# Softmax minus one-hot: each partition owns 64 neighbouring rows, and labels load straight into place

## The chip, the cores and the metric

The kernel runs on one core of one Trainium2 chip. The metric is the device time of one execution in microseconds (us). Before the change three runs took 1247.91, 1247.98 and 1248.11 us; the median is 1247.98 us.

## The reference

For 8 x 1024 = 8192 rows of 8192 float32 logits, the kernel computes the softmax of each row and subtracts 1.0 at the row's label. It is the gradient of the cross entropy with respect to the logits.

```python
logits_max = np.max(logits, axis=-1, keepdims=True)
exp_logits = np.exp(logits - logits_max)
softmax = exp_logits / np.sum(exp_logits, axis=-1, keepdims=True)
...
one_hot[batch_idx, seq_idx, labels] = 1.0
return (softmax - one_hot).astype(np.float32)
```

The labels are passed to the kernel as 64-bit integers. Logits in and gradient out are 268.4 MB each, so each byte of 537 MB is moved once.

## The kernel before

The rows are cut into B = 32 blocks of 256. In a block each of the 128 partitions holds G = 2 neighbouring rows, so block b and partition p hold the rows 256b + 2p and 256b + 2p + 1. One row of one partition is 32 KB. Partition p's rows of a block begin 64 KB after partition p-1's in HBM, and a block is one contiguous run of 8 MB. "Step t" below is one row of every partition (128 rows, 4 MB); there are T = 64 steps, two for each block.

SBUF holds three blocks (SLOTS = 3) in one tile `X` of 128 partitions x 3 slots x 2 rows x 8192 columns. Everything works in place in it. The order of all work is written out by hand: the helper `run` (line 63) issues one instruction, puts the waits on semaphores in front of it and increments a counter. As all instructions go through it, the profile shows L68 for nearly all of them, and they are told apart by engine, operation and tile.

Loads are issued by SyncE (SP) on queue q1. The string `LOADS` says for each block whether it is loaded as two DMAs of one row for each partition ("r", 128 pieces of 32 KB) or as one DMA of both rows ("w", 128 pieces of 64 KB): blocks 0 to 4 and 26 to 31 are "r", the 21 between are "w". A load of block b waits until the stores of block b-3, which used the same slot, have landed. Stores are issued by ScalarE (ACT) on queue q10, one for each step (128 pieces of 32 KB). Both directions run on the same 16 DMA engines.

For each step t the main loop (line 160) does this:

- VectorE (DVE) finds the negated row maximum (`tensor_reduce` into `m`), once the load has landed. It is issued one step ahead.
- ScalarE computes exp(x - max) in place and sums the row into `s`.
- VectorE takes the reciprocal into `r`.
- ScalarE multiplies the row by `r`.
- VectorE compares the tile `iota` (the column numbers, int16, in PSUM) with the row's label, and subtracts the result from the row (`scalar_tensor_tensor`). The label is a scalar for each partition, read from the tile `lab`.
- ScalarE issues the store of step t-1 between its two passes of step t.

Before the loop the constants are prepared. ScalarE issues the load of the labels (line 77) into `lab_raw`, with block b on partition b: 32 partitions x 256 labels. GpSimd (POOL) makes a 32x32 identity with a memset and an affine select (lines 78 to 83), and writes the column numbers with an iota into the last row of slot 2 of `X` (line 86), which is still empty. VectorE casts the labels to float (line 91). TensorE (PE) transposes them in two instructions into PSUM (line 93), one for each row j of a block, so that the labels of a partition's rows come to that partition. VectorE copies them into `lab` (line 97), laid out as [row j, block b], and copies the column numbers into PSUM (line 98). This last copy, `w_iota`, waits for the transposed labels, because they stood in the same PSUM tile, and for GpSimd's iota. The second load of block 2 (SP's sixth DMA) waits for it, since it overwrites the place where the column numbers were made, and VectorE's first row maximum stands behind it in VectorE's order.

Of the kernel before, what the change touches and what calls it, by code (L numbers as in the profile page):

```python
# [7 lines left out]
P = 128  # L8
G = 2
# [8 lines left out]
def kernel(  # L18
# [6 lines left out]
    nc = tc.nc  # L25
    fp32 = mybir.dt.float32
    i32 = mybir.dt.int32
    i16 = mybir.dt.int16
    Act = mybir.ActivationFunctionType
    Alu = mybir.AluOpType  # L30

    x_nv = logits.flatten_outer_dims()
    o_nv = out.flatten_outer_dims()
    N, V = x_nv.shape
    T = N // P
    B = T // G
    lab_bp = labels.rearrange("a b -> (a b)").rearrange("(b q) -> b q", q=G * P)
    x_b = x_nv.rearrange("(b p j) v -> b p j v", p=P, j=G)
    o_b = o_nv.rearrange("(b p j) v -> b p j v", p=P, j=G)

    const = ctx.enter_context(tc.tile_pool(name="const", bufs=1))
    psum = ctx.enter_context(tc.tile_pool(name="psum", bufs=1, space=bass.MemoryType.PSUM))


    X = const.tile([P, SLOTS, G, V], fp32)
    lab_raw = const.tile([B, G * P], labels.dtype)
    lab_f = const.tile([B, G, P], fp32)
    ident = const.tile([B, B], fp32)
    lab = const.tile([P, G, B], fp32)

    m, s, r = (const.tile([P, T], fp32, name=n) for n in ("m", "s", "r"))

    iota = psum.tile([P, V], i16)
    lab_ps = iota[:].bitcast(fp32)[:, :T].rearrange("p (j b) -> p j b", j=G)

    with tc.tile_critical():  # L56
        sem = tc.alloc_semaphore
        got = [[sem(f"got{i}{q}") for q in range(2)] for i in range(SLOTS)]
        put = [[sem(f"put{i}{q}") for q in range(2)] for i in range(SLOTS)]
        lab_got, dve, act, pe, pool = (sem(n) for n in ("lab_got", "dve", "act", "pe", "pool"))  # L60
        count = {}

        def run(engine, waits, counter, method, **operands):

            waits = list(dict.fromkeys(waits))
            for w in waits[:-1]:
                engine.wait_ge(*w)
            instruction = getattr(engine, method)(**operands)  # L68
            for w in waits[-1:]:
                instruction._wait_ge(*w)  # L70
            step = 16 if method == "dma_start" else 1
            instruction.then_inc(counter, step)
            count[counter.name] = count.get(counter.name, 0) + step
            return counter, count[counter.name]


        w_raw = run(nc.scalar, [], lab_got, "dma_start", out=lab_raw[:], in_=lab_bp)
        w = run(nc.gpsimd, [], pool, "memset", ap=ident[:], constant=0.0)
        w_ident = run(
            nc.gpsimd, [w], pool, "affine_select",  # L80
            out=ident[:], in_=ident[:], compare_op=Alu.not_equal, fill=1.0,
            base=0, pattern=[[-1, B]], channel_multiplier=1,
        )

        made = X[:, SLOTS - 1, G - 1, :].bitcast(i16)[:, :V]
        w_made = run(
            nc.gpsimd, [], pool, "iota", out=made, pattern=[[1, V]], base=0, channel_multiplier=0
        )
        step = mybir.dt.size(labels.dtype) // 4
        lab32 = lab_raw[:].bitcast(i32).rearrange("b (p j s) -> b j p s", j=G, s=step)  # L90
        w_lab = run(nc.vector, [w_raw], dve, "tensor_copy", out=lab_f[:], in_=lab32[:, :, :, 0])
        for j in range(G):
            w = run(
                nc.tensor, [w_ident, w_lab], pe, "transpose",
                out=lab_ps[:, j, :], in_=lab_f[:, j, :], identity=ident[:],
            )
        w_turned = run(nc.vector, [w], dve, "tensor_copy", out=lab[:], in_=lab_ps)
        w_iota = run(
            nc.vector, [w_turned, w_made], dve, "tensor_scalar",
            out=iota[:].bitcast(i32), in0=made.bitcast(i32), scalar1=0, scalar2=None, op0=Alu.bitwise_or,  # L100
        )

# [17 lines left out]
        def load(b):  # L120
            loaded[b] = []
            before = stored.get(b - SLOTS, last_made if b == SLOTS - 1 else [])
            for q, piece in enumerate(PIECES[LOADS[b]]):
                ps, js = piece
                free = [w for other, w in before if meets(piece, other)]
                w = run(
                    nc.sync, free, got[b % SLOTS][q], "dma_start",
                    out=X[ps, b % SLOTS, js, :], in_=x_b[b, ps, js, :],
                )
                loaded[b].append((piece, w))  # L130

        def store(t):
            b, j = divmod(t, G)
            stored.setdefault(b, [])
            for q, piece in enumerate(PIECES[STORES[b]]):
                ps, js = piece
                if js.stop != j + 1:
                    continue
                w = run(
                    nc.scalar, [finished[t]], put[b % SLOTS][q], "dma_start",  # L140
                    out=o_b[b, ps, js, :], in_=X[ps, b % SLOTS, js, :],
                )
                stored[b].append((piece, w))


        def row(t):
            return X[:, t // G % SLOTS, t % G, :]

        def row_max(t):
            b, j = divmod(t, G)  # L150
            arrived = [w for piece, w in loaded[b] if meets(piece, (every, slice(j, j + 1)))]
            return run(
                nc.vector, arrived, dve, "tensor_reduce",
                out=m[:, t : t + 1], in_=row(t), axis=mybir.AxisListType.X, op=Alu.max, negate=True,
            )
# [3 lines left out]
        w_max = row_max(0)  # L159
        for t in range(T):  # L160
            x = row(t)
            label = lab[:, t % G, t // G : t // G + 1]
            w = run(
                nc.scalar, [w_max], act, "activation",
                out=x, in_=x, func=Act.Exp, bias=m[:, t : t + 1], scale=1.0, accum_out=s[:, t : t + 1],
            )
            w_sum = run(nc.vector, [w], dve, "reciprocal", out=r[:, t : t + 1], in_=s[:, t : t + 1])
            if t + 1 < T:
                if (t + 1) % G == 0:
                    load((t + 1) // G)  # L170
                w_max = row_max(t + 1)
            if t > 0:
                store(t - 1)

            n = 1 if t + 1 < T else 2
            cols = [slice(i * V // n, (i + 1) * V // n) for i in range(n)]
            scaled = [
                run(
                    nc.scalar, [w_sum], act, "activation",
                    out=x[:, c], in_=x[:, c], func=Act.Copy, bias=0.0, scale=r[:, t : t + 1],  # L180
                )
                for c in cols
            ]
            for c, w in zip(cols, scaled):
                w = run(
                    nc.vector, [w], dve, "scalar_tensor_tensor",
                    out=x[:, c], in0=iota[:, c], scalar=label, in1=x[:, c],
                    op0=Alu.is_equal, op1=Alu.subtract, reverse1=True,
                )
            finished.append(w)  # L190
# [34 lines left out]
```

## Time and profile before

| | |
|---|---|
| median of three runs | 1247.98 us |
| span of the profiled execution, first to last instruction | 1245.7 us |
| median above the span | 2.3 us |
| bytes read and written in HBM | 268.50 MB and 268.44 MB |
| mean rate over the span | 431 GB/s |
| VectorE busy | 1119.2 us, 90% of the span |
| ScalarE busy | 919.1 us, 74% |
| GpSimd busy | 7.4 us |
| TensorE busy | 0.4 us |
| DMA from issue to landing: store, load of one row, load of two rows | 30.8, 26.6 and 33.4 us (medians) |

The times come from the runs, everything else from one execution that was recorded by the profiler. Its own time is its span with what lies around it, and that rest is not in the record; the table therefore sets the span against the median of the runs. A page of the profile has six parts: busy time of each engine, the span in 40 slices, the DMA queues, the chain of work that ended last, the groups of equal instructions with the idle time before them, and the DMA issues. The trace also has a record of each DMA packet, with its queue, size and duration; a packet carries one contiguous piece, and 4-byte packets signal completion.

### The profile page before, as it was taken

To read this page: it belongs to the slowest core of one execution; us is meant where nothing else is said; L and a number is where in the kernel's file an instruction comes from. 1 tells how busy PE (TensorE), PEld (TensorE's weight loads), DVE (VectorE), ACT (ScalarE), POOL (GpSimd) and SP (SyncE) were. 2 spreads that over 40 slices of the span, in tenths; PEclk is the share of its full clock that TensorE was granted. 3 is DMA by queue.
4 is the path that set the end of the run, shared out by engine and by line. 5 is a ranking of instruction groups with operands and counts; after the bars stand their busy time and mean duration, and the time that the engine had idled before them with its cause. 6 is when DMAs were issued, how large, how long until landed. Compare 5 with 4: busy or idle time off the path is not lost.

```text
span 1245.7 us, 592 instructions
## 1 busy us (share of the span) xinstructions
PE 0.4 (0%) x2; PEld 0.3 (0%) x2; DVE 1119.2 (90%) x196; ACT 919.1 (74%) x194; POOL 7.4 (1%) x7
## 2 busy tenths in 40 slices
PE   0000000000000000000000000000000000000000
PEld 0000000000000000000000000000000000000000
DVE  5999998888988889888998888988889999999893
ACT  3888886778776787767877778777777788887772
POOL 2000000000000000000000000000000000000000
DMA  9999999999999999999999999999999999999998
GB/s 406 417 429 433 438 433 442 437 426 427 430 435 445 439 417 442 426 430 437 432 443 438 420 435 432 430 437 450 420 426 437 436 428 432 437 435 429 432 437 386
DMA packets 15460, 536.98 MB, mean 431 GB/s; under 512 B 1728, under 2 KB 1728, under 8 KB 1760
## 3 DMA queue, kind: packets, MB, share of 16 engines
q1 hardware_dynamic: 6192, 268.44, 50.0%
q10 hardware_dynamic: 9264, 268.51, 49.9%
q14 instruction: 4, 0.03, 0.0%
HBM read 268.50 MB, written 268.44 MB: 431 GB/s over the span
## 4 chain that ended last, share of the span: by engine, by line
DMA 59%; DVE 37%; another core or an unknown queue 2%; ACT 1%; DVEq 0%; issue 0%; PE 0%; SPq 0%; ACTq 0%
DMA X<-in_logits_dram 31%; DMA out_dram<-X 27%; DVE m L68 18%; DVE X L68 18%; ACT X L68 1%; DVE iota L68 0%; DVEq L56 0%; DMA lab_raw<-in_labels_dram 0%; DVE lab_f L68 0%; DVE r L68 0%; PE iota L68 0%; SPq L68 0%; ACTq L68 0%; DVE lab L68 0%
## 5 line engine op out<-in xcount | busy, mean ns | idle before, releaser
L68 DVE TENSOR_REDUCE m<-X 128x1 f32<-128x8192 f32 x64 | 555.2, 8675 | 94.3 <-DMA X<-in_logits_dram 94.3
L68 ACT ACTIVATE X<-X,m 128x8192 f32<-128x8192 f32 x64 | 455.9, 7123 | 188.4 <-DVE m L68 188.4
L68 DVE SCALAR_TENSOR_TENSOR X<-iota,lab,X 128x8192 f32<-128x8192 int16 (+1 forms) x65 | 559.7, 8612 | 4.1 <-ACT X L68 4.1
L68 ACT ACTIVATE X<-X,r 128x8192 f32<-128x8192 f32 (+1 forms) x65 | 456.0, 7017 | 115.9 <-DVE r L68 115.9
L68 DVE RECIPROCAL r<-s 128x1 f32<-128x1 f32 x64 | 9.9, 154 | 7.3 <-ACT X L68 7.3
L68 ACT ACTIVATION_READ_ACCUMULATOR X<-X,m 128x1 f32 x64 | 12.0, 187 | 0.0
L68 DVE CAST lab_f<-lab_raw 32x256 f32<-32x256 int32 x1 | 3.7, 3685 | 4.7 <-DMA lab_raw<-in_labels_dram 4.7
L68 POOL IOTA X<- 128x8192 int16 x1 | 6.9, 6944 | 0.0
L68 DVE TENSOR_SCALAR iota<-X 128x4096 int32<-128x4096 int32 x1 | 4.4, 4427 | 0.1
L68 ACT ACT_TABLE_LOAD x1 | 1.3, 1283 | 1.3 <-SPq L56 1.3
L68 DVE COPY lab<-iota 128x64 f32<-128x64 f32 x1 | 0.2, 225 | 0.5 <-PE iota L68 0.5
L68 PE MATMUL iota<-ident,lab_f 32*128 32x32 f32 x2 | 0.4, 300 | 8.5 <-DVE lab_f L68 8.5
L68 PEld LDWEIGHTS iota<-ident,lab_f 32*128 32x128 f32 x2 | 0.3, 196 | 8.4 <-DVE lab_f L68 8.4
L68 POOL TENSOR_SCALAR_AFFINE_SELECT ident<-ident 32x32 f32<-32x32 f32 x1 | 0.2, 204 | 0.1
L68 POOL MEMSET ident<- 32x32 f32 x1 | 0.1, 115 | 0.5 <-SPq L56 0.5
L209 POOL MEMSET const-bfloat16-1.0<- 128x1 bf16 x1 | 0.1, 107 | 0.0
L209 POOL MEMSET const-uint8-127<- 128x1 uint8 x1 | 0.1, 107 | 0.0
L209 POOL MEMSET const-float32-0.0<- 128x1 f32 x1 | 0.1, 104 | 0.2 <-issue 0.2
L209 POOL MEMSET const-float32-1.0<- 128x1 f32 x1 | 0.1, 104 | 0.0
## 6 DMA issues: line engine op xcount, KB each, us to landing
out_dram<-X ACTq DMA_DIRECT2D x64, 4096.0 KB, 30.8
X<-in_logits_dram SPq DMA_DIRECT2D x22, 4096.0 KB, 26.6
X<-in_logits_dram SPq DMA_DIRECT2D x21, 33.4
lab_raw<-in_labels_dram ACTq DMA_DIRECT2D x1, 64.0 KB, 3.8
```

The source lines that it names most:

```text
L68: instruction = getattr(engine, method)(**operands)
L209: nc = _bacc.Bacc("TRN2", target_bir_lowering=False, num_devices=1)
```

## The change

Partition p now owns the 64 neighbouring rows 64p to 64p + 63 (2 MB of HBM), and block b takes the rows 64p + 2b and 64p + 2b + 1 of each partition. Loads, stores, their sizes, their order and their waits stay; their addresses in HBM change. The labels of a partition's rows are 64 neighbouring numbers, so one DMA puts them on their partitions (128 partitions x 64 labels, 512 B each), and one cast brings them into `lab`, now in the order of the steps. The identity, the transposes, their PSUM view and the copy out of PSUM are dropped, and with them the semaphore `pe`.

```diff
-    lab_bp = labels.rearrange("a b -> (a b)").rearrange("(b q) -> b q", q=G * P)
-    x_b = x_nv.rearrange("(b p j) v -> b p j v", p=P, j=G)
-    o_b = o_nv.rearrange("(b p j) v -> b p j v", p=P, j=G)
+    lab_pt = labels.rearrange("a b -> (a b)").rearrange("(p t) -> p t", p=P)
+    x_b = x_nv.rearrange("(p b j) v -> b p j v", p=P, j=G)
+    o_b = o_nv.rearrange("(p b j) v -> b p j v", p=P, j=G)
...
-    lab_raw = const.tile([B, G * P], labels.dtype)
-    lab_f = const.tile([B, G, P], fp32)
-    ident = const.tile([B, B], fp32)
-    lab = const.tile([P, G, B], fp32)
+    lab_raw = const.tile([P, T], labels.dtype)
+    lab = const.tile([P, T], fp32)
...
-    lab_ps = iota[:].bitcast(fp32)[:, :T].rearrange("p (j b) -> p j b", j=G)
...
-        w_raw = run(nc.scalar, [], lab_got, "dma_start", out=lab_raw[:], in_=lab_bp)
-        w = run(nc.gpsimd, [], pool, "memset", ap=ident[:], constant=0.0)
-        w_ident = run(
-            nc.gpsimd, [w], pool, "affine_select",
-            out=ident[:], in_=ident[:], compare_op=Alu.not_equal, fill=1.0,
-            base=0, pattern=[[-1, B]], channel_multiplier=1,
-        )
+        w_raw = run(nc.scalar, [], lab_got, "dma_start", out=lab_raw[:], in_=lab_pt)
...
-        lab32 = lab_raw[:].bitcast(i32).rearrange("b (p j s) -> b j p s", j=G, s=step)
-        w_lab = run(nc.vector, [w_raw], dve, "tensor_copy", out=lab_f[:], in_=lab32[:, :, :, 0])
-        for j in range(G):
-            w = run(
-                nc.tensor, [w_ident, w_lab], pe, "transpose",
-                out=lab_ps[:, j, :], in_=lab_f[:, j, :], identity=ident[:],
-            )
-        w_turned = run(nc.vector, [w], dve, "tensor_copy", out=lab[:], in_=lab_ps)
+        lab32 = lab_raw[:].bitcast(i32).rearrange("p (t s) -> p t s", s=step)
+        w_lab = run(nc.vector, [w_raw], dve, "tensor_copy", out=lab[:], in_=lab32[:, :, 0])
         w_iota = run(
-            nc.vector, [w_turned, w_made], dve, "tensor_scalar",
+            nc.vector, [w_lab, w_made], dve, "tensor_scalar",
...
-            label = lab[:, t % G, t // G : t // G + 1]
+            label = lab[:, t : t + 1]
```

More of the change, by code (lines that the diff above doesn't have):

```diff
@@ L59 @@
         put = [[sem(f"put{i}{q}") for q in range(2)] for i in range(SLOTS)]
-        lab_got, dve, act, pe, pool = (sem(n) for n in ("lab_got", "dve", "act", "pe", "pool"))
+        lab_got, dve, act, pool = (sem(n) for n in ("lab_got", "dve", "act", "pool"))
         count = {}
```

## The prediction

> **What bounds the kernel now.** I read the page from the bottom up: first the DMA queues (part 3) and the slices (part 2), then the chain of work that ended last (part 4), then the groups (part 5).
>
> ```profile
> DMA  9999999999999999999999999999999999999998
> GB/s 406 417 429 433 438 433 442 437 426 427 430 435 445 439 417 442 426 430 437 432 443 438 420 435 432 430 437 450 420 426 437 436 428 432 437 435 429 432 437 386
> ...
> q1 hardware_dynamic: 6192, 268.44, 50.0%
> q10 hardware_dynamic: 9264, 268.51, 49.9%
> ...
> DMA 59%; DVE 37%; another core or an unknown queue 2%; ACT 1%; DVEq 0%; issue 0%; PE 0%; SPq 0%; ACTq 0%
> ```
>
> The loads (q1) and the stores (q10) each take half of all sixteen DMA engines' time: 99.9% together. No slice has slack. VectorE's 37% of the chain is not a second bound. In the groups its row maxima stand idle for 94.3 us in front of loads:
>
> ```profile
> L68 DVE TENSOR_REDUCE m<-X 128x1 f32<-128x8192 f32 x64 | 555.2, 8675 | 94.3 <-DMA X<-in_logits_dram 94.3
> ...
> L68 DVE CAST lab_f<-lab_raw 32x256 f32<-32x256 int32 x1 | 3.7, 3685 | 4.7 <-DMA lab_raw<-in_labels_dram 4.7
> L68 POOL IOTA X<- 128x8192 int16 x1 | 6.9, 6944 | 0.0
> L68 DVE TENSOR_SCALAR iota<-X 128x4096 int32<-128x4096 int32 x1 | 4.4, 4427 | 0.1
> ```
>
> So the time is bytes divided by what the DMA engines move, and the question is how long a packet takes. In the trace's packet records a packet is one piece of a partition: 32 KB for one row (2816 loads, 8192 stores), 64 KB for two (2688 loads). Median: 1213 ns for 32 KB, 2418 ns for 64 KB. Added over the records and divided by 16 engines, loads take 621.9 us, stores 621.1 us, together 1243.0 us of the 1245.7 us span; 2.7 us are left for the start, the completion packets (9 ns each) and the labels. The median run of 1247.98 us lies 2.3 us above the profiled span, and I keep these 2.3 us.
>
> If every packet had its median, loads would fall by 2.1 us. **Nothing in the data path can gain more than about 2 us** unless 1213 ns itself falls, and in no record does a 32 KB packet take less.
>
> **The start, part by part.**
>
> *Removed:* on GpSimd a memset (115 ns) and an affine select (204 ns); on TensorE two transposes with their weight loads (0.43 us in the chain); on VectorE one copy (225 ns). These stood in the chain from the labels' landing (4.69 us) to the iota copy's start (9.25 us).
>
> *Changed:* the cast turns from 32x256 into 128x64. The old one took 3685 ns, far above the 225 ns of the 128x64 copy beside it, and ended at 8.40 us, 0.15 us after GpSimd's iota (1.31 to 8.25 us). The trace doesn't say whether the iota held it up. Bounds for the new one: 0.2 us to 3.7 us. It hardly matters: the iota copy also waits for GpSimd's iota, which starts some 0.35 us earlier and ends at about 7.9 us; labels plus cast end between 4.9 and 8.4 us. So the iota copy starts at 7.9 to 8.4 us instead of 9.25, and ends at 12.3 to 12.8 instead of 13.67.
>
> *What is late next:* the first load. It was issued at 0.96 us and took 12.2 us to land, so row 0 is there at 13.2 us. The first maximum can move from 13.6 to 13.2 us and no further: 0.4 us. Behind it only SP's sixth load waits for the iota copy (10.1 us of SP's waiting). Five loads of 4 MB are ahead of it in the queue, 20.97 MB, or 49 us at 431 GB/s; issued 1 us earlier it lands no earlier. As the DMA engines are full to the end, the 0.4 us don't reach the end of the program: I take 0, bounds 0 and -0.4 us.
>
> *Labels:* the same 64 KB come as 128 packets of 512 B instead of 32 of 2 KB. A 2 KB packet took 81 to 315 ns (mean 114), a 4 B packet 9. The 96 more packets cost each engine between 6 x 9 ns = 0.05 us and 6 x 114 ns = 0.7 us: I take 0.3 us. If that delays the labels from 4.7 to 5.4 us, GpSimd's iota still covers it.
>
> *Unmoved:* SP's and ACT's issues stand in the old order with the old waits; every load has its old shape and count, so the packets keep their sizes (the two rows of a 64 KB packet remain neighbours in HBM).
>
> The start is thus worth -0.4 to +0.7 us, 0.3 us taken.
>
> **The address of every packet.** This is the change that counts, and the trace of before has no row for it. Partition p's packet used to lie 64 KB behind that of partition p-1; a block was one run of 8 MB. Now it lies 64 rows x 32 KB = 2 MB behind it, in loads and in stores. All packets of a DMA start at addresses that differ by multiples of 2 MB, so if HBM serves some addresses in turn and not side by side, sixteen engines at the same offset now meet there, and go on meeting in every packet.
>
> The nearest rows are the two places where loads were slow in before. The first sixteen load packets, one for each engine, started within 0.67 us and took 1372 to 2113 ns, mean 1673: 1673/1213 = 1.38. At 48 to 52 us, just after the first store had been issued, 32 load packets took 1380 to 2279 ns, mean 1794: 1.48. The windows show both as a dip while the engines stay busy:
>
> ```profile
> 2.00:4.00 2.00, 0.00 (x0) 0.00 (x0) 0.00 (x0) 0.63 (x1) 2.00 (x1) 1.00 1.04 337
> ...
> 48.00:50.00 2.00, 0.00 (x0) 0.00 (x0) 2.00 (x1) 2.00 (x1) 0.00 (x0) 1.00 0.94 262
> 50.00:52.00 2.00, 0.00 (x0) 0.00 (x0) 2.00 (x1) 2.00 (x1) 0.00 (x0) 1.00 0.86 262
> ...
> 200.00:900.00 700.00, 0.00 (x0) 0.00 (x0) 627.12 (x110) 517.15 (x109) 0.00 (x0) 1.00 1.00 434
> ```
>
> (The last two columns are the DMA share and GB/s.) Stores were never slow: the longest of 8192 took 1291 ns. Bounds for the 2 MB distance are therefore 1.00 (as in nearly all rows) and 1.48 on every packet. I take the row of engines that start together, 1.38, for loads, and 1.00 for stores, because that is how the rows divide. **Sum:** 621.9 x 1.38 + 621.1 + 2.7 + 0.3 + 2.3 = 858.2 + 626.4 = **1484.6 us**. The computing engines stay below: VectorE's 1119 us would be 75% of it.
>
> The Trainium skill has a rule here that speaks against this change: "DMA: Bandwidth & Descriptors", section "Latency and other measured facts", says that copies between HBM tensors whose partitions lie a large power of two apart lose rate, 164 GB/s in each direction at 2 MiB against 214 in full. By these figures the estimate is 1243.0 x 214/164 + 5.3 = 1627 us. No run here shows that distance yet.
>
> **Rivals.**
>
> *A, loads slow, stores not (forecast), 0.52.* For: the division of the rows. Against: after the first round the sixteen engines still start within some 0.7 us of each other and take 1213 ns, so standing in step is not enough at a distance of 64 KB, and the first packets may have been slow for being first. With a factor of 1.10 to 1.60 instead of 1.38 it gives 1310 to 1621 us.
>
> *B, loads and stores both slow, 0.19.* For: both now have the same 2 MB distance, and both queues are active from 47 us to the end. Against: no slow store in before. Price: 1243.0 x 1.38 + 5.3 = 1721 us, from about 1600. The Trainium skill's rule named above is of this kind, as its copies slow in both directions.
>
> *C, no effect, 0.24: the other side, not slower.* HBM has room for the 434 GB/s wherever the packets lie, and the DMA engines stay the bound. For: packets at two distances from each other (loads of one region, stores of another) mix for 1100 us at exactly 1213 ns, as if the limit were in the engine. It decides from the point where a 2 MB packet takes 1213 ns: then 1243.0 + 2.7 + 0.3 + 2.3 = 1248.3 us, 1247 to 1249 with the bounds of the start.
>
> *D, the start counts after all, 0.02.* The slow first packets vanish (2 us) and the 0.4 us reach the end: 1245.3 us.
>
> *E, worse than B, 0.03:* 1.48 or more everywhere: 1845 us.
>
> The change may also not do what it says: if the cast still ends only with GpSimd's iota, the labels' shorter way gains nothing. That is inside C's bounds.
>
> **How the numbers follow.** 0.2% is 2.5 us, about what a measurement of this kernel can tell from no change. Faster by more is D's better half and a remainder: 0.02. Within 0.2%: C, less a tail: 0.22. Slower: A, B, E and that tail: 0.76. The likeliest is A, 1485 us, own range 1310 to 1621. The range takes in C below and A, with B's lowest part, above: 1246 to 1640 us; outside are most of B, E and part of D, 0.2.
>
> **What would show it.** If A is right, part 3 gives q1 a share well above q10's; GB/s falls to some 360 in all slices, the DMA digits stay at 9; a load packet takes about 1.67 us and a store packet 1.21; VectorE's idle before the row maxima grows from 94 to over 300 us. If B is right, both shares stay near 50% and GB/s falls to 310. If C is right, the GB/s row looks as before. In each case the first TENSOR_REDUCE begins when row 0 lands (A: about 16 us, from eight packets of 1673 ns instead of one; C: 13.2), GpSimd's iota ends near 7.9 us, and the transposes and the second copy are gone. The prediction is wrong if slices early (loads only) and late differ much, or if a second store-side effect appears: then the distance isn't what sets the packet's time. It would also be wrong in size if only some blocks slowed, as the offset within the 2 MB moves on by 64 KB with each block.

## The result, and the profile after

The changed kernel takes 1462.82 us (median of four runs, 1462.18 to 1464.0), the kernel before 1247.97 us beside it: a ratio of 1.172, 95% interval 1.171 to 1.174. It is slower by 215 us. The prediction's 1485 us lies 22 us above.

The page of the changed kernel, the same lines as before: slices, DMA queues, chain.

```profile
DMA  9999999999999999999999999999999999999997
GB/s 350 353 377 379 418 360 349 359 372 382 377 347 335 381 338 367 351 353 335 357 356 343 368 332 379 372 388 369 324 366 363 394 383 396 407 413 399 391 401 315
...
q1 hardware_dynamic: 6192, 268.44, 53.1%
q10 hardware_dynamic: 9360, 268.51, 45.1%
...
DMA 65%; DVE 26%; another core or an unknown queue 7%; ACT 1%; DVEq 0%; SPq 0%; issue 0%; ACTq 0%
```

The bytes and the loads' packets are the same, and the DMA digits still read 9, but the rate fell from about 431 to 367 GB/s. In the chain, DMA grew from 59% to 65% and VectorE shrank from 37% to 26%. A busy engine says nothing about how fast it moves: the packets last longer. Loads now hold a larger share than stores (53.1% against 45.1%), so they suffer more. The two shares add up to 98.2% instead of 99.9%: for some 26 us of the span the engines now have nothing to do.

The groups of the changed kernel (line, engine, operation, operands, count; busy time and mean; idle before and its cause):

```profile
L65 DVE TENSOR_REDUCE m<-X 128x1 f32<-128x8192 f32 x64 | 555.3, 8676 | 306.4 <-DMA X<-in_logits_dram 306.4
...
L65 DVE CAST lab<-lab_raw 128x64 f32<-128x64 int32 x1 | 0.2, 196 | 11.7 <-DMA lab_raw<-in_labels_dram 11.7
L65 POOL IOTA X<- 128x8192 int16 x1 | 7.0, 6953 | 0.6 <-PEq L205 0.6
L65 DVE TENSOR_SCALAR iota<-X 128x4096 int32<-128x4096 int32 x1 | 4.4, 4427 | 0.1
```

No instruction on VectorE takes longer. The row maxima wait 306.4 us for loads instead of 94.3, and that difference of 212 us is the loss seen from VectorE. The cast is short, but it stands behind labels that land at 11.7 us instead of 4.7.

The windows of the changed kernel (length, busy time of VectorE, ScalarE and GpSimd, clock, DMA share, GB/s) separate the loads-only start from the mixed part, in which stores run too:

```profile
4.00:20.00 16.00, 8.16 (x3) 0.00 (x0) 3.99 (x1) 1.00 0.97 373
20.00:46.00 26.00, 18.72 (x4) 19.22 (x4) 0.00 (x0) 1.00 1.00 382
60.00:130.00 70.00, 70.00 (x13) 58.10 (x13) 0.00 (x0) 1.00 1.00 360
200.00:900.00 700.00, 499.82 (x86) 410.54 (x86) 0.00 (x0) 1.00 0.98 358
1230.00:1420.00 190.00, 160.07 (x28) 135.40 (x28) 0.00 (x0) 1.00 1.00 402
```

The row of the kernel before for its loads-only start, with two more columns in front, for TensorE:

```profile
20.00:40.00 20.00, 0.00 (x0) 0.00 (x0) 12.72 (x4) 16.01 (x4) 0.00 (x0) 1.00 0.98 421
```

Loads alone are slow already (382 GB/s from 20 to 46 us, against 421); with stores beside them it gets worse (358, where the kernel before has 434); the last stretch, where loads come in 32 KB pieces again, is better (402). The length of the pieces is not all of it, though: from 60 to 130 us the loads are 32 KB pieces too, and the rate is 360. These differences led to the experiments.

"Engine time" below is the sum of the 32 and 64 KB packet records of a direction divided by 16 engines, as in the prediction. It went from 621.9 to 776.2 us for loads (x1.25) and from 621.1 to 658.8 us for stores (x1.06). The slowness is uneven: 39% of the load packets still take their old time, and 17% more than 1.5 times as much. The longest 64 KB load took 6.9 us, the longest store 3.8 us.

### The profile page after: what moved, and what is told of

It reads as the page before. It is cut to its first block, busy times and chain, and to the rows that moved or that the text cites. A ratio compares the mean times of both kernels' runs of the same rounds, so it can differ in the third digit from the quotient of the medians.

```text
span 1461.4 us, 580 instructions
## 1 busy us (share of the span) xinstructions
DVE 1116.3 (76%) x195; ACT 919.0 (63%) x194; POOL 7.2 (0%) x5
## 3 DMA queue, kind: packets, MB, share of 16 engines
q1 hardware_dynamic: 6192, 268.44, 53.1%
q10 hardware_dynamic: 9360, 268.51, 45.1%
## 4 chain that ended last, share of the span: by engine, by line
DMA 65%; DVE 26%; another core or an unknown queue 7%; ACT 1%; DVEq 0%; SPq 0%; issue 0%; ACTq 0%
DMA X<-in_logits_dram 33%; DMA out_dram<-X 30%; DVE m L65 13%; DVE X L65 13%; ACT X L65 1%; DMA lab_raw<-in_labels_dram 1%; DVE iota L65 0%; DVEq L53 0%; SPq L65 0%; DVE r L65 0%; ACTq L65 0%; DVE lab L65 0%; ACTq L205 0%; DVEq L64 0%
## 5 line engine op out<-in xcount | busy, mean ns | idle before, releaser
L65 DVE TENSOR_REDUCE m<-X 128x1 f32<-128x8192 f32 x64 | 555.3, 8676 | 306.4 <-DMA X<-in_logits_dram 306.4
L65 DVE CAST lab<-lab_raw 128x64 f32<-128x64 int32 x1 | 0.2, 196 | 11.7 <-DMA lab_raw<-in_labels_dram 11.7
## 6 DMA issues: line engine op xcount, KB each, us to landing
lab_raw<-in_labels_dram ACTq DMA_DIRECT2D x1, 64.0 KB, 10.8
```

## The experiments

The theory to start from: the 2 MB between the pieces of a DMA is the whole loss, and it slows each DMA by its own pieces. The rivals: the labels' late landing, or far stores that burden all loads. Some of these kernels put the one-hot or the output into other rows; only their times count here. Twelve kernels ran; each was timed beside the kernel before on the same chip (1247.9 to 1248.3 us).

### Which half of the change

**The labels' path alone.** The changed kernel with the old addresses for logits and output:

```diff
-    x_b = x_nv.rearrange("(p b j) v -> b p j v", p=P, j=G)
-    o_b = o_nv.rearrange("(p b j) v -> b p j v", p=P, j=G)
+    x_b = x_nv.rearrange("(b p j) v -> b p j v", p=P, j=G)
+    o_b = o_nv.rearrange("(b p j) v -> b p j v", p=P, j=G)
```

> The labels' new path alone: rows lie as before the change, so the one-hot lands in the wrong rows. Theory 1 (the distance of 2 MB between the partitions' pieces is the whole loss): within 0.2% of before, 1246 to 1250 us, packets of 1213 ns in loads and stores. Theory 2 (the labels' late landing, 11.7 us after the change against 4.7 before, shifts the order of loads and stores for good, and this costs): over 1300 us. Either way the first row maximum starts where the labels allow it; if the eight small packets of an engine each wait behind one load packet, the labels land at 10 to 12 us here too, though load packets are fast, and the maximum starts near 16 us.

Measured: 1248.18 us, ratio 1.0000 (0.9991 to 1.0009). The timeline of its start (start, duration, what):

```profile
1.04 6.95 POOL L65 IOTA X<- 128x8192 int16 x1 [0.60 <-PEq L205]
...
9.69 0.20 DVE L65 CAST lab<-lab_raw 128x64 f32<-128x64 int32 x1 [9.69 <-DMA lab_raw<-in_labels_dram]
10.00 4.43 DVE L65 TENSOR_SCALAR iota<-X 128x4096 int32<-128x4096 int32 x1
14.33 8.68 DVE L65 TENSOR_REDUCE m<-X 128x1 f32<-128x8192 f32 x1
```

The labels land late here too, at 9.69 us, though load packets are fast; the first maximum starts at 14.33 us instead of 13.58, not near the 16 us that were expected. Neither shows in the total. The packet records give the reason for the late landing: 64 label packets start within the first 1.1 us of the loads, and the other 64 in four bursts of 16, 1.23 us apart, one packet for each engine. Each small packet takes its turn with a 32 KB load packet (1213 ns) of the other queue. An engine used to have two label packets and now has eight. The Trainium skill, "DMA: Bandwidth & Descriptors", section "Queues, rings and completion order", says that an engine goes round its queues packet by packet, and that a packet typically holds some 9 to 17 descriptors (single moves). The trace agrees on the turns, but here a turn held a single 512 B piece.

**The rows alone.** The kernel before with the new addresses, labels still transposed:

```diff
-    x_b = x_nv.rearrange("(b p j) v -> b p j v", p=P, j=G)
-    o_b = o_nv.rearrange("(b p j) v -> b p j v", p=P, j=G)
+    x_b = x_nv.rearrange("(p b j) v -> b p j v", p=P, j=G)
+    o_b = o_nv.rearrange("(p b j) v -> b p j v", p=P, j=G)
```

> The new rows alone, with the labels still transposed (they then belong to other rows, so the one-hot lands wrongly). Theory 1: as after the change, 1455 to 1470 us, loads about 1.25 and stores about 1.06 of their packets' time before. Theory 2: near 1248 us.

Measured: 1462.73 us, ratio 1.172 (1.170 to 1.175); engine time 780.4 us for loads, 655.3 us for stores. The rows are the whole loss. The rival about the labels has fallen.

### Loads or stores

**Far loads, near stores**: in the changed kernel the stores' addresses are put back.

```diff
-    o_b = o_nv.rearrange("(p b j) v -> b p j v", p=P, j=G)
+    o_b = o_nv.rearrange("(b p j) v -> b p j v", p=P, j=G)
```

> Only the loads' pieces lie 2 MB apart, the stores' 64 KB as before (so the output's rows are permuted). Theory 1a (a packet is slow by the distance within its own DMA): loads 1.25, stores 1.00, some 777 + 621 us of engine time, about 1400 us in all. Theory 1b (loads are slow because far stores keep HBM busy; loads suffer from the stores' distance): near 1250 to 1290 us.

**Far stores, near loads**: the loads' addresses are put back instead.

```diff
-    x_b = x_nv.rearrange("(p b j) v -> b p j v", p=P, j=G)
+    x_b = x_nv.rearrange("(b p j) v -> b p j v", p=P, j=G)
```

> Only the stores' pieces lie 2 MB apart, the loads' 64 KB (the output's rows are permuted). Theory 1a: loads 1.00, stores 1.06, about 1285 us. Theory 1b: loads remain at about 1.25 though their own pieces are near, about 1400 us or more.

Far loads alone: 1322.55 us, ratio 1.060 (1.057 to 1.062). Far stores alone: 1319.88 us, 1.058 (1.055 to 1.060). The queues of the kernel with far loads, then of the one with far stores:

```profile
q1 hardware_dynamic: 6192, 268.44, 51.5%
q10 hardware_dynamic: 9360, 268.51, 47.6%
```

```profile
q10 hardware_dynamic: 9360, 268.51, 51.3%
q1 hardware_dynamic: 6192, 268.44, 48.4%
```

In both the far direction holds more of the engines. Engine time is 680.7 us for far loads beside 629.5 us for near stores, and 672.7 us for far stores beside 635.7 us for near loads. Both sharp forms of the theory missed: by 1a far loads would have cost 154 us and far stores 38, by 1b far loads next to nothing. What is seen is that each direction pays for its own distance, 59 and 52 us of engine time, and the other pays 8 and 14 us. The two losses of 74 and 72 us add up to 146 us, and both together cost 215: 69 us come only from the combination. In engine time the loads carry more than all of it: they take 776 us instead of 681 when the stores become far as well, while the far stores take less beside far loads than beside near ones (659 instead of 673).

**Another offset between the streams.** Blocks are stored half a partition further on:

```diff
-                    out=o_b[b, ps, js, :], in_=X[ps, b % SLOTS, js, :],
+                    out=o_b[(b + B // 2) % B, ps, js, :], in_=X[ps, b % SLOTS, js, :],
```

> The changed kernel, but each block's rows are stored 16 blocks (1 MB) further on, modulo the partition's 2 MB, so that load and store streams stand at another offset to each other (the output's rows are permuted). Far loads alone cost 74 us and far stores alone 72 us, both together 215. Theory S (the 69 us on top come from loads and stores that meet on the same part of HBM because they go through the 2 MB two blocks apart): the time changes by more than 20 us, towards 1248 + 146 = 1394 us. Theory N (they come from sharing what the far rows leave of HBM's rate, wherever the streams stand): 1450 to 1475 us.

Measured: 1440.28 us, ratio 1.154 (1.151 to 1.158). It moved by 22 us, a third of the 69, which is just enough for theory S by its own bound of 20 us and far from its 1394 us, and outside the range of theory N. The four runs (1435 to 1447 us) lie on both sides of that bound. The offset between loads and stores matters some; most of the combined loss stays, and where it comes from is open.

### Which distance

The rows were taken in C parts, one after the other, so that the partitions' pieces lie 2 MB / C apart:

```diff
-    x_b = x_nv.rearrange("(p b j) v -> b p j v", p=P, j=G)
+    x_b = x_nv.rearrange("(c p b j) v -> c b p j v", c=C, p=P, j=G)
...
-                    out=X[ps, b % SLOTS, js, :], in_=x_b[b, ps, js, :],
+                    out=X[ps, b % SLOTS, js, :], in_=x_b[b * C // B, b % (B // C), ps, js, :],
```

and the same for `o_b`. The expectations for 1 MB, 512 KB and 256 KB:

> Distance of 1 MB: the blocks go over the first half of the rows, then over the second (the one-hot falls in wrong rows). Theory P: the loss shrinks with the power of two, since twice as many different places are met; estimate about half of the 215 us, 1355 us, bounds 1260 and 1463. Theory D: little less than at 2 MB, over 1400 us.

> Distance of 512 KB between 256 KB (5 us lost) and 1 MB (115 us lost); the one-hot falls in wrong rows. Theory P with a loss that halves from 2 MB to 1 MB (215 to 115 us) and then falls faster: 1270 to 1310 us. If there is a threshold at 1 MB instead: below 1260 us.

> Distance of 256 KB (the one-hot falls in wrong rows). Theory P: almost no loss, 1248 to 1265 us. Theory D: the loss falls with the logarithm of the distance, at two fifths of the way from 64 KB to 2 MB: about 1330 us.

A distance that is not a power of two, 62 rows, was made in this way (`o_b` alike):

```diff
-    x_b = x_nv.rearrange("(p b j) v -> b p j v", p=P, j=G)
+    x_b = [x_nv[: N - G * P].rearrange("(p b j) v -> b p j v", p=P, j=G)[i] for i in range(B - 1)]
+    x_b.append(x_nv[N - G * P :].rearrange("(p j) v -> p j v", j=G))
```

> 31 of the 32 blocks use a distance of 62 rows (1984 KB, 31 x 64 KB) between the partitions' pieces in place of 64 rows (2048 KB); the last block takes the 256 rows left over, 64 KB apart. Nothing else differs from the change (the one-hot falls in wrong rows, as the labels are loaded as in the changed kernel). Theory P (the loss comes from distances that are a large power of two, so that all pieces of a DMA and both streams fall on the same part of HBM): 1247 to 1252 us, all packets 1213 ns. Theory D (any large distance costs, as the pieces of a DMA are spread over 256 MB): 1450 to 1470 us.

| distance between partitions | us | ratio to before (95%) | engine time: loads, stores (us) |
|---|---|---|---|
| 64 KB (before) | 1247.97 | 1 | 621.9, 621.1 |
| 256 KB | 1252.87 | 1.004 (1.003 to 1.005) | 625.2, 622.2 |
| 512 KB | 1286.54 | 1.031 (1.029 to 1.032) | 648.0, 626.7 |
| 1 MB | 1363.32 | 1.091 (1.085 to 1.096) | 701.6, 640.7 |
| 2 MB (changed kernel) | 1462.82 | 1.172 (1.171 to 1.174) | 776.2, 658.8 |
| 1984 KB (62 rows) | 1249.61 | 1.001 (1.000 to 1.002) | 622.3, 621.2 |

The last row decides: 1984 KB is nearly as far as 2048 KB and costs nearly nothing. Slices and queues of that kernel:

```profile
DMA  9999999999999999999999999999999999999998
GB/s 405 418 429 432 437 435 439 433 429 428 431 432 448 433 420 434 431 441 435 422 450 435 418 429 433 437 439 428 427 437 435 429 432 436 433 430 433 436 432 384
...
q1 hardware_dynamic: 6192, 268.44, 50.0%
q10 hardware_dynamic: 9360, 268.51, 49.9%
```

This is nearly the page of before again: 39 of the 40 slices lie within 11 GB/s of it. Distance as such (theory D) is no cause; the loss belongs to distances that are large powers of two (theory P) and grows with them: 5, 39, 115 and 215 us, the first three within the bounds of theory P. 62 rows is the one other distance that was tried; a multiple of 512 KB that is no power of two, such as 1.5 MB, was not. Nor does any run show what the packets meet on in HBM: that part of theory P is argued. The Trainium skill, "DMA: Bandwidth & Descriptors", section "Latency and other measured facts", has 207 GB/s at a pitch of 512 KiB where 214 is the full rate, a factor of 1.034; the 1.031 measured here agrees. At 2 MiB its figures make 1.305, and here 1.172 was measured, which decides for this kernel. Its copies went from HBM to HBM in pieces of 16 KiB, this kernel moves 32 and 64 KB pieces to and from SBUF; which of these makes the difference was not tried.

### The size of the pieces

**One-row loads only**, in the changed kernel and, as a control, in the kernel before:

```diff
-LOADS = "rrrrrwwwwwwwwwwwwwwwwwwwwwrrrrrr"
+LOADS = "rrrrrrrrrrrrrrrrrrrrrrrrrrrrrrrr"
```

> The changed kernel with every block loaded as two DMAs of one row (pieces of 32 KB) in place of the 21 blocks of 64 KB pieces. In the changed kernel 64 KB load packets took 1.29 of their old time, 32 KB ones of the last blocks 1.16. Theory L (long pieces suffer more, as two engines that meet stay together longer): loads fall to 1.16, 720 us instead of 776, about 1410 us in all. Theory N (the size of a piece doesn't matter; the last blocks are faster for another reason, as the loads lie elsewhere in the 2 MB or the stores are fewer): 1450 to 1480 us.

> The control for the run with one-row loads only: the kernel before the change (64 KB between partitions, labels transposed) with every block loaded as two DMAs of 32 KB pieces. If short pieces help only against the far rows (theory L), this stays within 0.5% of before, 1246 to 1254 us. If short load pieces help as such, because loads and stores then take turns of equal size, it falls below 1245 us; the DMA engines' 1243 us of packets leave hardly room for that.

With far rows: 1358.50 us, ratio 1.089 (1.086 to 1.093). With near rows: 1248.04 us, 1.0001 (0.9991 to 1.0010). The middle of the far kernel with one-row loads, to be read against 358 GB/s in the same stretch of the changed kernel:

```profile
200.00:900.00 700.00, 578.22 (x101) 476.15 (x102) 0.00 (x0) 1.00 1.00 400
```

The loads' engine time falls to 721.4 us, as expected by theory L (720). The total falls by 104 us, twice what was expected, since the stores recover too (658.8 to 628.7 us) and the engines' idle time shrinks: the profiled execution's own time less both engine times is 28.2 us in the changed kernel (1463.2 us) and 15.9 us here (1366.0 us, the longest of the four runs). So the string of load shapes, without effect on near rows, is worth half the loss on far ones.

The packets of the kernels with one far direction mostly agree. With far loads alone, 64 KB loads took 1.13 of their old time and 32 KB loads 1.04. With far stores alone, the stores took 1.11 of their old time while 64 KB loads ran (173 to 1025 us); beside the near 32 KB loads they took 1.08 before that stretch and 1.00 behind it.

Whether long pieces hurt by their length, because loads then hold an engine for twice as long a turn as stores, or because a load of two rows waits for two stores and a load of one row for one, these runs don't separate.

### A version without the loss

It has the distance of 62 rows, and SP issues the labels ahead of the first load on its own queue, in two DMAs: each partition's first 62 labels, then its last 2 (T - G = 62; `lab_pt` and `lab_pj` are these two parts):

```diff
-        w_raw = run(nc.scalar, [], lab_got, "dma_start", out=lab_raw[:], in_=lab_pt)
+        run(nc.sync, [], lab_got, "dma_start", out=lab_raw[:, : T - G], in_=lab_pt)
+        w_raw = run(nc.sync, [], lab_got, "dma_start", out=lab_raw[:, T - G :], in_=lab_pj)
```

> A complete version with the far rows' harm taken out: distance of 62 rows for 31 blocks, the last 256 rows as one block 64 KB apart, labels loaded straight into place without transposes by two small DMAs (496 B and 16 B pieces) that SP issues ahead of the first load on its own queue. Theory Q (in the changed kernel the labels landed late, at 11.7 us, because each of an engine's 8 small packets took its turn with a load packet of the other queue): the labels land within 3 to 5 us, the iota copy starts as GpSimd's iota ends, at about 8 us, and the first maximum starts when row 0 has landed, 13 to 14.5 us. If they land late for another reason (their 128 small pieces), still after 9 us. The total stays with before in either case, 1246 to 1251 us, as the DMA engines are full.

Measured: 1249.27 us, ratio 1.0012 (1.0003 to 1.0020). The timeline of its start:

```profile
0.95 0.85 SPq L69 DMA_DIRECT2D lab_raw<-in_labels_dram  x2
1.04 6.95 POOL L69 IOTA X<- 128x8192 int16 x1 [0.59 <-PEq L210]
1.85 11.08 SPq L69 DMA_DIRECT2D X<-in_logits_dram  x6
3.08 4.96 DVE L69 CAST lab<-lab_raw 128x64 f32<-128x64 int32 x1 [3.08 <-DMA lab_raw<-in_labels_dram]
8.15 4.43 DVE L69 TENSOR_SCALAR iota<-X 128x4096 int32<-128x4096 int32 x1
14.37 8.69 DVE L69 TENSOR_REDUCE m<-X 128x1 f32<-128x8192 f32 x1 [1.79 <-DMA X<-in_logits_dram]
```

The labels land at 3.08 us, though they are 256 small packets now: it was the turns with the other queue that delayed them (theory Q). VectorE then waits 1.79 us for row 0, in part because the first load was issued 0.9 us later. The whole preparation is off the path, as the total shows: this version takes the labels without transposes and takes 0.1% longer than the kernel before. The DMA engines' 1243 us leave no room to beat it.

## Why the prediction was right, point by point

**The bound** was right: the time stayed that of the DMA engines. Of the 215 us, 192 are longer packets and the other 23 time between packets, in which the engines are idle. The labels alone, which the sum put at 0.3 us, are not to be told from before (1248.18 us).

**The loads** were the mis-sized term: 621.9 x 1.38 = 858.2 us by the prediction, 776.2 us measured, a factor of 1.25. **The stores** were taken at 1.00 and came out at 1.06, 658.8 us. **The rest** was taken as 5.3 us and is 27.9 us, the median less both engine times, because the engines no longer stay full. The three errors are -82.0, +37.7 and +22.6 us, together -21.7: that is how 1484.6 became 1462.8. The total is closer than its terms, so some of it is luck. (Loads at their median packet would have saved 2.2 us before the change, not 2.1; nothing rests on it.)

**The row behind 1.38** measured something else. The first sixteen load packets, in order of start, take 1679 ns on average at 62 rows too, where nearly nothing else is lost, against 1673 ns before the change; so they are slow for being first, as the case against the forecast said. Nor do they follow the distance: with 2 MB between the loads' pieces they took 1378 ns (far loads alone), 1760 (changed kernel) and 2031 (rows alone). And in the changed kernel packets don't slow evenly: 39% keep their time, and a few take up to 3.8 times as long. The row gave the right sign and, by chance, a size of the right order, 1.38 for 1.25.

**The rivals.** B, both directions slow by 1.38, didn't come, but its core was there: stores are slowed by their own distance (1.08 alone in far stores). The forecast's split by direction rested on rows at 64 KB and hides that either direction alone costs the same, 74 and 72 us. C (no effect) is what 62 rows give. The start (D) stayed hidden.

**The signs to look for** held in part 3 (q1 above q10), in the rate (367 GB/s against some 360), in the digits at 9 and in VectorE's idle (306.4 us against "over 300"). "All slices" was too simple: the slices run from 315 to 418. A load packet takes 1.44 us on average for 32 KB, not 1.67, and 3.11 us for 64 KB; a store packet takes 1.29 us on average, not 1.21. Two of the prediction's signs of being wrong came as well. A store-side effect appeared, and the rate differed between stretches (382, 358 and 402 GB/s). So the time came out near the forecast and the larger part of the loss lies in the loads, but the split "loads slow, stores not" was wrong: the distance acts on both directions, and it does not alone set a packet's time, since the length of the load pieces changes the loss too.

**The start** failed in one step: the labels were to land at 5.4 us at the latest, hidden behind GpSimd's iota, and the iota copy to start at 7.9 to 8.4 us. They landed at 11.7, and it started at 12.04 us. The sum counted the small packets' own time and not the turns that they wait for. The first maximum began at 16.37 us, near the 16 us named, but it was the iota copy that released it. Row 0, the reason given, had landed at 15.9 us (0.96 + 14.9).

## What to carry to other kernels

Where the DMA engines are the bound, a layout is a change of every packet's duration: work out the distance between the pieces that are in flight together, and when it is a power of two of 512 KB or more, expect a loss (3%, 9% and 17% here at 512 KB, 1 MB and 2 MB) and try a distance a little off it, as 1984 KB was here, before giving up the layout. The DMA digits of the page stay at 9 through all of this; read GB/s and the packets' time instead. A small DMA issued beside a stream of large ones pays one large packet for each of its own on an engine, so put it ahead of the stream on the same queue.

## What the runs showed of the hardware that was not expected

- Far loads and far stores cost 74 and 72 us alone and 215 us together; another 1 MB of offset between them changed that by 22 us.
- 32 KB instead of 64 KB load pieces took half of the loss away at a distance of 2 MB (215 to 110 us) and changed nothing at 64 KB.
- A VectorE cast of 128x64 took 196 ns after GpSimd's iota had ended, and 4960 ns when it was issued at 3.08 us during the iota, ending at 8.04 us just after it (7.99). The 3685 ns of the cast before the change look like the same wait: it ended at 8.40 us, the iota at 8.25. What holds the cast up, no run here shows.
- 128 label packets of 512 B last 27 ns each at the median and take 8.8 to 10.8 us to land beside a load stream; ahead of it, two DMAs of 128 small packets land in 1.7 and 1.9 us.
